# A two-block transformer kernel on one core: expert choosing paced by VectorE's estimated lead, cut into two-head pieces, and expert weighing handed out one chunk sooner

## The chip, the cores and the metric

The kernel runs on one core of one Trainium2 chip. The metric is device time in microseconds (us); the time of a kernel is the median of its runs. The engines are TensorE (PE: matmuls; PEld: its weight loads), VectorE (DVE), ScalarE (ACT), GpSimd (POOL) and SyncE (SP), which here only issues the loads of weights. TensorE's granted clock is shown as a share of its full 2.4 GHz.

## The reference

The reference computes two transformer blocks on 256 tokens of width 2048 in fp32. The change touches the feed-forward part of the first block, a layer of 16,384 experts from which each of 8 heads chooses 16 per token:

```python
def peer(x, w_query, sub_keys, expert_down, expert_up):
    q = (xt @ w_query).reshape(T, PEER_HEADS, 2, PEER_HALF)
    scores = jnp.einsum('thpc,hpnc->thpn', q, sub_keys)
    vals, idx = lax.top_k(scores, PEER_TOPK)
    cand = (vals[..., 0, :, None] + vals[..., 1, None, :]).reshape(T, PEER_HEADS, 256)
    top_vals, top_c = lax.top_k(cand, PEER_TOPK)
    i1 = jnp.take_along_axis(idx[..., 0, :], top_c // PEER_TOPK, axis=-1)
    i2 = jnp.take_along_axis(idx[..., 1, :], top_c % PEER_TOPK, axis=-1)
    experts = (i1 * PEER_N_KEYS + i2).reshape(T, PEER_HEADS * PEER_TOPK)
    gates = jax.nn.softmax(top_vals, axis=-1)
    ...
        u = jnp.take(expert_down, ec, axis=0)
        hdn = jax.nn.gelu(jnp.einsum('ted,td->te', u, xc))
        return jnp.einsum('te,ted->td', gc * hdn, jnp.take(expert_up, ec, axis=0))
```

## The kernel before, in words

**Dense experts.** The kernel does not gather experts. It computes gelu(x · expert_down) for all 16,384 experts, multiplies it by a gate that is zero where an expert wasn't chosen, and multiplies the product by expert_up. Every weight matrix is streamed once from HBM, and TensorE works through them in one long list of matmul stages.

**Steps.** A weight tile of 1 MB (`raw`, 3 buffers, loaded by SP) is worked in two halves. One half is a *step*, the variable `s` of the loop in `run` (L265); this text numbers steps by it. An fp32 product is made of three products of rounded operands, so each half is split: ScalarE copies it to `whi` (rounded), VectorE subtracts `raw - whi` into `wlo`. Both have 4 buffers, and the split of step s + 3 (`LOOK = 3`) is issued in step s. TensorE then runs the matmuls of step s. The query projection of the expert layer is steps 128 to 159; the expert_down stage, called s1, has 16 chunks of 1024 experts and is steps 160 to 415; the expert_up stage, s2, is steps 416 to 671. A step has 12 wide matmuls (512 columns) in the query stage and in s2, and the equal of 16 in s1.

**Evacuations.** Every 4 steps of s1 the accumulator is full and `s1_evac` (L919) empties it: ScalarE copies (`tmp<-acc`), VectorE adds and multiplies (`tmp<-tmp,acc`, `tmp<-tmp,nb`), ScalarE applies gelu and issues a store to HBM (`act`). These are issued at the end of steps 163, 167, ..., 415. The next steps' `whi` stand behind the gelu in ScalarE's order, and the `wlo` behind them.

**Side work.** The order of instructions on every engine is the order in which the program issues them. Work beside the matmuls is written as generators in named *lanes*; at the end of every step, `round` (L222) advances each running generator of each lane by one piece. The lanes that matter here:

- "top": `query` (L975) for a group of two heads and 128 tokens: transposes, key scores, and `top16` of 128 scores for two heads and two halves (MAX8, FIND_INDEX8, MATCH_REPLACE8 on VectorE).
- "choose": `choose` (L1016), for 4 heads and 128 tokens: candidate sums (14 small adds), top16 of 50 candidates, then for each head two pieces of compare, multiply and reduce over 128x400 to recover the ids (`eq`), and a softmax with one Exp on ScalarE. There are 4 of these.
- "rows": `scatter` (L1084). For each of 64 columns of a `choose`, GpSimd issues an indirect DMA that adds gates into one of four gate tensors in HBM (two halves of the heads, two of the tokens). There are 256 in all.
- "main": `weigh` (L1112), once per chunk. It waits, while the program is being written, until all scatters are issued, three of seven 8 KB `nb` buffers are free and it is at most one chunk ahead of the last one that was finished. Then GpSimd issues the loads of the chunk's activations and of four gate pieces and adds the head halves (`nb<-nb,nb`, 2 adds); after 5 rounds VectorE multiplies activations by gates (2 multiplies), and the result is split into the operand `xt` of s2.

The first `weigh` is handed to its lane at the last evacuation of chunk 14 (step 399).

**Estimates.** `Meter` (L171) adds up an estimated time `vt` for every engine as instructions are issued, kept from falling more than 2.0 us behind TensorE's. In `split`, a `wlo` is put on GpSimd instead of VectorE when VectorE's estimate leads:

```python
busy = self.vt["DVE"] - self.vt["PE"] > self.share and self.vt["POOL"] - self.vt["PE"] < 1.0
```

`share` is 2.0, and out of reach (1e9) from the first scatter issued to the last.

Of the kernel before, what the change touches and what calls it, by code (L numbers as in the profile page):

```python
# [8 lines left out]
F32 = mybir.dt.float32  # L9
# [4 lines left out]
OP = mybir.AluOpType  # L14
# [11 lines left out]
NCAND = 50  # L26
CLAMP = 2.0
SWA_ORDER = [0, 3, 1, 4, 2, 5, 6, 9, 7, 10, 8, 11]

# [142 lines left out]
class Meter:  # L172
# [5 lines left out]
    def __getattr__(self, op):  # L178
        f = getattr(self.eng, op)
        if "dma" in op or op == "preload_act_table_set":  # L180
            return f

        def g(*a, **k):
            out = a[0] if a else k["out"]
            n = 1
            for d in out.shape[1:]:
                n *= d
            per = self.per
            if self.name == "PE" and k.get("rhs", a[2] if len(a) > 2 else out).dtype == F32 and op == "matmul":
                per = 4 * per  # L190
            vt = self.vt
            vt[self.name] = max(vt[self.name], vt["PE"] - CLAMP if self.name != "PE" else 0.0) + self.fixed + n * per
            return f(*a, **k)  # L193
        return g


class Engines:
    def __init__(self, nc):
        self.vt = vt = dict(PE=0.0, DVE=0.0, ACT=0.0, POOL=0.0)
        self.tensor = Meter(nc.tensor, "PE", vt, 0.0, 0.000417)  # L200
        self.vector = Meter(nc.vector, "DVE", vt, 0.085, 0.00104)
        self.scalar = Meter(nc.scalar, "ACT", vt, 0.2, 0.00083)
        self.gpsimd = Meter(nc.gpsimd, "POOL", vt, 0.1, 0.00225)
        self.sync = nc.sync


class Build:
# [6 lines left out]

    def lane(self, name, width, starts=1):

        self.lanes[name] = dict(width=width, starts=starts, queue=deque(), active=[])

# [3 lines left out]
    def round(self):  # L222
        for ln in self.lanes.values():
            st = 0
            while ln["queue"] and len(ln["active"]) < ln["width"] and st < ln["starts"]:
                ln["active"].append([self.now, ln["queue"].popleft()])
                st += 1
            for item in list(ln["active"]):
                if item[0] <= self.now:
                    try:  # L230
                        w = next(item[1])
                        item[0] = self.now + (1 if w is None else w)
                    except StopIteration:
                        ln["active"].remove(item)
        self.now += 1
# [338 lines left out]
    def body(self):  # L574
        from contextlib import ExitStack
        with ExitStack() as ctx:
# [16 lines left out]
            self.lane("attn", 2, 1)  # L593
            self.lane("top", 1, 1)
            self.lane("choose", 1, 1)
            self.lane("rows", 4, 2)
# [285 lines left out]
    def peer(self, hn, st):  # L882
        nc, ins = self.nc, self.ins
# [23 lines left out]
        def q_evac(g, acc):  # L907
            for tt in range(2):
                self.until(lambda: st["q"])
                q = st["q"].popleft()  # L910
                nc.scalar.activation(q, acc[tt], AF.Copy, scale=st["rh"][:, tt:tt + 1])
                self.add("top", self.query(g, tt, q, st, topn))
            if g % 2:
                for tt in range(2):
                    self.add("choose", self.choose(g // 2, tt, st, topn, done))

        def s1_evac(c):
            def f(g, acc):
# [11 lines left out]
                if j == 3:  # L930
                    ws.append(self.weigh(c, acts, at, st, done, s2))
                    if c >= nch - 2:
                        while ws:
                            self.add("main", ws.pop(0))
# [80 lines left out]

    def choose(self, hf, tt, st, topn, done):  # L1016

        nc, p = self.nc, self.pp
        while (2 * hf, tt) not in topn or (2 * hf + 1, tt) not in topn:
            yield 1  # L1020
        hs = slice(4 * hf, 4 * hf + 4)
# [3 lines left out]
        cand = p.tile([128, 2, 4, NCAND], F32, name="cand", tag="cand", bufs=1)  # L1025
        ec = cand[:, 1]
        cand = cand[:, 0]
        eng = nc.vector
        for src, dst in ((v, cand), (ixf, ec)):
            o = 0  # L1030
            for a, na, nb in CAND:
                x0 = src[:, :, 0, a:a + na]
                x1 = src[:, :, 1, 0:nb]
                d = dst[:, :, o:o + na * nb]
                if na == 1:
                    eng.tensor_tensor(d, x0.to_broadcast([128, 4, nb]), x1, op=OP.add)
                elif nb == 1:
                    eng.tensor_tensor(d, x0, x1.to_broadcast([128, 4, na]), op=OP.add)
                else:
                    eng.tensor_tensor(d.rearrange("p h (a b) -> p h a b", a=na),  # L1040
                                      x0[:, :, :, None].to_broadcast([128, 4, na, nb]),
                                      x1[:, :, None, :].to_broadcast([128, 4, na, nb]), op=OP.add)
                o += na * nb
        yield 1
        tt4 = p.tile([128, 6, 4, 16], F32, name="tt4", tag="tt4", bufs=1)
        tv, tf, tp, e, gs = tt4[:, 0], tt4[:, 1], tt4[:, 2].bitcast(U32), tt4[:, 3], tt4[:, 4]
        for h in range(4):
            self.top16(cand[:, h, :], tv[:, h, :], tp[:, h, :])
            yield 1
        nc.vector.tensor_copy(tf, tp)  # L1050

        cs = slice(64 * hf, 64 * hf + 64)
        gt = st["pk"][:, tt, 1, cs].rearrange("p (h j) -> p h j", h=4)
        nc.vector.tensor_tensor(gt, tv, tv[:, :, 0:1].to_broadcast([128, 4, 16]), op=OP.subtract)
        nc.scalar.activation(gt, gt, AF.Exp)
# [7 lines left out]
        for h in range(4):  # L1063
            for j in (slice(0, 8), slice(8, 16)):
# [9 lines left out]
        nc.vector.reciprocal(gs[:, :, 1], gs[:, :, 0])  # L1074
        nc.vector.tensor_tensor(gt, gt, gs[:, :, 1:2].to_broadcast([128, 4, 16]), op=OP.mult)
# [4 lines left out]
        if hf == 1 and tt == 1:  # L1080
            self.nb.give(st["top"])
        self.add("rows", self.scatter(hf, tt, st, done))

    def scatter(self, hf, tt, st, done):  # L1084

        nc = self.nc
        gd = st["gd"][hf, tt].rearrange("e (t o) -> (e t) o", o=1)
# [6 lines left out]
        done["rows"] += 64  # L1094
        if done["rows"] == T:
# [16 lines left out]
    def weigh(self, c, acts, at, st, done, s2):  # L1112
# [592 lines left out]
```

## Time and profile before

| | us |
|---|---|
| median of 3 runs | 3170.18 (3170.11 to 3171.86) |
| the profiled execution, its own time | 3169.29 |
| its span in the trace | 3167.5 |
| TensorE busy in the span | 3076.1 (97%) |
| query projection, about | 460 to 545 |
| s1, about | 545 to 1328 |
| s2, from | 1328 |

Rows of the trace are read so: a row of instructions has the line, engine, operation, `out<-in` by the program's names, the count, then busy time and mean duration, and last the idle time of that engine just before, with what ended it. In a timeline the first number is the start in us, the second how long the group took. A row of waits says which engine waited, in which line, for whom, how long in total, how often and how long at most. Nearly all operations are recorded under one line (L193), as they pass through a helper, so the names of tiles tell them apart.

### The profile page before, as it was taken

To read this page: it belongs to the slowest core of one execution; us is meant where nothing else is said; L and a number is where in the kernel's file an instruction comes from. 1 tells how busy PE (TensorE), PEld (TensorE's weight loads), DVE (VectorE), ACT (ScalarE), POOL (GpSimd) and SP (SyncE) were. 2 spreads that over 40 slices of the span, in tenths; PEclk is the share of its full clock that TensorE was granted. 3 is DMA by queue.
4 is the path that set the end of the run, shared out by engine and by line. 5 is a ranking of instruction groups with operands and counts; after the bars stand their busy time and mean duration, and the time that the engine had idled before them with its cause. 6 is when DMAs were issued, how large, how long until landed. Compare 5 with 4: busy or idle time off the path is not lost.

```text
span 3167.5 us, 38904 instructions
## 1 busy us (share of the span) xinstructions
PE 3076.1 (97%) x15388; PEld 2576.2 (81%) x15388; DVE 2019.2 (64%) x2821; ACT 1438.3 (45%) x1908; POOL 748.2 (24%) x502
## 2 busy tenths in 40 slices
PE   8999999789999999789999999999999999999998
PEld 6888888678888888668888888877888888888887
DVE  5555667997555555657777765655757555555565
ACT  4444454444444444424444444554555444444444
POOL 3011200267888863433122200000111000000000
PEclk9999999999999999989999999999999999999999
DMA  9556954457777777778777755554444455555554
GB/s 348 216 178 222 330 180 173 137 165 201 209 211 211 212 210 241 279 264 280 263 269 267 278 203 187 185 203 139 170 172 169 172 192 188 194 190 186 189 194 149
DMA packets 157527, 667.28 MB, mean 211 GB/s; under 512 B 48945, under 2 KB 65757, under 8 KB 90145
## 3 DMA queue, kind: packets, MB, share of 16 engines
q1 hardware_dynamic: 77984, 551.64, 48.5%
q0 software_dynamic: 61808, 96.32, 12.4%
q10 hardware_dynamic: 17552, 16.85, 1.6%
q8 instruction: 120, 1.97, 0.2%
q14 instruction: 63, 0.51, 0.0%
HBM read 612.16 MB, written 54.94 MB: 211 GB/s over the span
## 4 chain that ended last, share of the span: by engine, by line
PE 86%; DVE 7%; DMA 3%; ACT 2%; issue 1%; POOL 1%; ACTq 0%; DVEq 0%; SPq 0%; POOLq 0%
PE acc L193 81%; PE aux L193 5%; DVE wlo L193 3%; DMA nb<-gates 2%; DVE nb L193 1%; ACT whi L193 1%; DVE tt L193 1%; DVE tmp L193 1%; DVE eq L193 1%; POOL nb L193 0%; DVE xt L193 0%; ACT tmp L193 0%; DMA raw<-in_w 0%; POOL nb L1121 0%; DMA raw<-in_wu 0%
## 5 line engine op out<-in xcount | busy, mean ns | idle before, releaser
L193 DVE TENSOR_TENSOR wlo<-raw,whi 128x1024 fp32r<-128x1024 f32 x1039 | 1303.6, 1261 | 896.4 <-ACT whi L193 895.6
L193 PE MATMUL acc<-whi,xt 128*128 128x512 f32 x5248 | 1668.1, 394 | 1.9 <-ACT whi L193 1.6
L193 ACT ACTIVATE whi<-raw 128x1024 fp32r<-128x1024 f32 x1040 | 1088.3, 1056 | 1052.8 <-PE acc L193 969.8
L193 PEld LDWEIGHTS acc<-whi,xt 128*128 128x128 f32 x5248 | 987.9, 188 | 215.3 <-issue 6.0
L193 PE MATMUL acc<-xt,whi 128*128 128x512 f32 x3072 | 1086.3, 400 | 1.0 <-DVE xt L193 1.0
L193 PE MATMUL acc<-wlo,xt 128*128 128x512 f32 x2624 | 1025.1, 391 | 21.6 <-DVE wlo L193 11.4
L193 PE MATMUL acc<-xt,wlo 128*128 128x256 f32 x3072 | 853.5, 283 | 45.7 <-DVE wlo L193 44.0
L193 PEld LDWEIGHTS acc<-xt,whi 128*128 128x128 f32 x3072 | 576.2, 189 | 133.8 <-DVE xt L193 1.2
L193 PEld LDWEIGHTS acc<-xt,wlo 128*128 128x128 f32 x3072 | 584.6, 190 | 61.7 <-DVE wlo L193 51.3
L193 PEld LDWEIGHTS acc<-wlo,xt 128*128 128x128 f32 x2624 | 494.7, 189 | 124.7 <-DVE wlo L193 14.3
L1090 POOL DMA_INDIRECT gates<-nb x256 | 476.5, 1861 | 413.3 <-DVE nb L193 231.4
L193 POOL TENSOR_TENSOR nb<-nb,nb 128x1024 f32<-128x1024 f32 (+1 forms) x34 | 98.1, 2901 | 197.2 <-DMA nb<-gates 172.6
L193 ACT ACTIVATE tmp<-tmp 128x512 f32<-128x512 f32 (+5 forms) x84 | 46.5, 554 | 179.4 <-DVE tmp L193 179.2
L1121 POOL DMA_DIRECT2D nb<-gates x64 | 56.9, 921 | 146.5 <-DVE xt L193 93.7
L193 ACT ACTIVATE tmp<-acc 128x256 f32<-128x256 f32 x128 | 47.1, 385 | 90.6 <-PE acc L193 90.6
L193 DVE TENSOR_TENSOR h<-h,acc 128x512 f32<-128x512 f32 x136 | 86.8, 679 | 0.0
L193 ACT ACTIVATE p<-p 128x128 f32<-128x128 f32 x88 | 39.4, 449 | 81.7 <-DVE p L193 81.7
L193 DVE TENSOR_TENSOR nb<-nb,nb 128x1024 f32<-128x1024 f32 (+2 forms) x42 | 61.2, 1465 | 23.6 <-POOL nb L193 23.6
L193 ACT ACTIVATE xt<-aux 128x512 fp32r<-128x512 f32 (+2 forms) x70 | 40.1, 583 | 79.4 <-PE aux L193 77.6
L193 DVE TENSOR_TENSOR tmp<-tmp,acc 128x256 f32<-128x256 f32 x128 | 49.2, 419 | 25.9 <-ACT tmp L193 25.9
L193 POOL TENSOR_TENSOR tmp<-nb,const 128x64 f32<-128x64 f32 x32 | 11.2, 379 | 229.4 <-ACT nb L193 229.4
L193 DVE TENSOR_TENSOR xt<-nb,xt 128x1024 fp32r<-128x1024 f32 x48 | 58.5, 1221 | 8.8 <-ACT xt L193 8.8
(232 smaller groups left out, 1253.4 us busy)
## 6 DMA issues: line engine op xcount, KB each, us to landing
raw<-in_wd SPq DMA_DIRECT2D x128, 1024.0 KB
raw<-in_wu SPq DMA_DIRECT2D x128, 1024.0 KB
raw<-in_wm SPq DMA_DIRECT2D x128, 1024.0 KB
raw<-in_w SPq DMA_DIRECT2D x87, 1024.0 KB
gates<-const POOLq DMA_DIRECT2D x32, 1024.0 KB
raw<-in_wo SPq DMA_DIRECT2D x32, 1024.0 KB
nb<-gates POOLq DMA_DIRECT2D x64, 512.0 KB
raw<-in_wq SPq DMA_DIRECT2D x16, 1024.0 KB
```

What stands on the lines that cost most here:

```text
L193: return f(*a, **k)
L1090: nc.gpsimd.indirect_dma_start(out=gd, out_offset=bass.IndirectOffsetOnAxis(ap=st["pk"][:, tt, 0, c:c + 1].bitcast(I32), axis=0), in_=st[" ...
L1121: nc.gpsimd.dma_start(g[:, :, 128 * tt:128 * tt + 128], st["gd"][hf, tt][CH * c:CH * c + CH].rearrange("(a p) t -> p a t", p=128))
```

## The change

1. **Estimates.** The size counted for an instruction is the largest of its operands instead of its output's. Each matmul gets 0.0133 us on top; VectorE's fixed and per-column estimates change slightly, and `max_index` and `match_replace` get 0.09 us on top.
2. **Pausing.** Lanes can be `paced`: their generators are not advanced in a round in which VectorE's estimate leads TensorE's by more than 2.0 us. "choose" and "top" are paced; "choose" now comes first, and "top" may run two generators.
3. **Choosing for two heads.** `choose` takes the two heads of one query group instead of four, so that there are 8 of them, each followed by 32 scatters instead of 64.
4. **Weighing.** The first `weigh` is handed out at the end of chunk 13 (step 383) instead of 14, and `weigh` waits 9 rounds instead of 5 between GpSimd's adds and VectorE's multiplies.

```diff
+MATCH, PACE = 0.09, 2.0
...
-            out = a[0] if a else k["out"]
             n = 1
-            for d in out.shape[1:]:
-                n *= d
+            for x in (a[:1] or (k["out"],)) if self.name == "PE" else (*a, *k.values()):
+                if len(getattr(x, "shape", ())) > 1:
+                    n = max(n, math.prod(x.shape[1:]))
...
+            vt[self.name] += MATCH if op in ("max_index", "match_replace") else 0.0
...
-        self.tensor = Meter(nc.tensor, "PE", vt, 0.0, 0.000417)
-        self.vector = Meter(nc.vector, "DVE", vt, 0.085, 0.00104)
+        self.tensor = Meter(nc.tensor, "PE", vt, 0.0133, 0.000417)
+        self.vector = Meter(nc.vector, "DVE", vt, 0.08, 0.00113)
...
-                if item[0] <= self.now:
+                if item[0] <= self.now and not (ln["paced"] and self.vt["DVE"] - self.vt["PE"] > PACE):
...
-            self.lane("top", 1, 1)
-            self.lane("choose", 1, 1)
+            self.lane("choose", 1, 1, True)
+            self.lane("top", 2, 2, True)
...
-            if g % 2:
-                for tt in range(2):
-                    self.add("choose", self.choose(g // 2, tt, st, topn, done))
+                self.add("choose", self.choose(g, tt, st, topn, done))
...
-                    if c >= nch - 2:
+                    if c >= nch - 3:
...
-    def choose(self, hf, tt, st, topn, done):
+    def choose(self, g, tt, st, topn, done):
...
-        while (2 * hf, tt) not in topn or (2 * hf + 1, tt) not in topn:
+        while (g, tt) not in topn:
...
-        for h in range(4):
+        for h in range(2):
...
-        for c in range(64 * hf, 64 * hf + 64):
+        for c in range(32 * g, 32 * g + 32):
...
-        yield 5
+        yield 9
```

Three places show what it moves in the orders of the engines.

**GpSimd, from the last zeroing of the gates to the first scatters** (`wlo` is the split of a weight half; `gates_188` and `gates_189` are two of the four gate tensors). Before, and then with the change:

```order
L896 DMA nb_12_3629<-in_keys 128x2048
L1108 DMA gates_191<-const 2048x1x128
L1090 DMA gates_188<-nb_14_3632 2097152x1 x15
L1090 DMA gates_189<-nb_14_3632 2097152x1
L1090 DMA gates_188<-nb_14_3632 2097152x1
```

```order
L1109 DMA gates_191<-const 2048x1x128
L195 TENSOR_TENSOR wlo<-raw,whi 128x1024 x7
L1091 DMA gates_188<-nb_14_3632 2097152x1 x9
L1091 DMA gates_189<-nb_14_3632 2097152x1
L1091 DMA gates_188<-nb_14_3632 2097152x1
```

Seven splits have moved from VectorE to GpSimd, ahead of its first scatter (they are issued in steps 139 to 141 and 146 to 149). The first scatter is issued in step 150 instead of 169, the last in step 258 instead of 278.

**VectorE, around an evacuation in s1 while choosing goes on** (`eq`, `cand` and `tt` belong to `choose`; `tmp` to the evacuation, `wlo` to the splits). Before, and then with the change:

```order
L193 TENSOR_TENSOR wlo<-raw,whi 128x1024
L193 TENSOR_TENSOR tmp<-tmp,acc 128x256 x2
L193 TENSOR_TENSOR tmp<-tmp,nb_14_3632 128x512
L193 TENSOR_REDUCE tt_4335<-eq_5_4546 128x8
L193 TENSOR_TENSOR eq_7_4616<-const,tt_4335 128x400
L193 TENSOR_TENSOR eq_7_4616<-eq_7_4616,cand 128x400
L193 TENSOR_TENSOR wlo<-raw,whi 128x1024
```

```order
L195 TENSOR_REDUCE tt_5296<-eq_18_5424 128x8
L195 TENSOR_TENSOR eq_20_5480<-const,tt_5296 128x400
L195 TENSOR_TENSOR eq_20_5480<-eq_20_5480,cand 128x400
L195 TENSOR_TENSOR wlo<-raw,whi 128x1024
L195 TENSOR_TENSOR tmp<-tmp,acc 128x256 x2
L195 TENSOR_TENSOR tmp<-tmp,nb_14_3632 128x512
L195 TENSOR_TENSOR wlo<-raw,whi 128x1024
```

Before, pieces of choosing stood between an evacuation and the next split; now the split follows at once. Of the 15 evacuations of steps 163 to 219, 1 was followed by a split at once before, and 12 are now. The last `choose` ends in step 227 instead of 215.

**VectorE, at the first multiplies of `weigh`** (`nb<-nb,nb`; `xt` is the operand of s2). Before, from the evacuation of step 403; with the change, from that of step 391:

```order
L193 TENSOR_TENSOR tmp<-tmp,acc 128x256 x2
L193 TENSOR_TENSOR tmp<-tmp,nb_14_3632 128x512
L193 TENSOR_TENSOR wlo<-raw,whi 128x1024
L193 TENSOR_TENSOR nb_15_10698<-nb_15_10698,nb_16_10699 128x1024
L193 TENSOR_TENSOR wlo<-raw,whi 128x1024
L193 TENSOR_TENSOR nb_15_10698<-nb_15_10698,nb_16_10699 128x1024
L193 TENSOR_TENSOR nb_18_10732<-nb_18_10732,nb_19_10733 128x1024
```

```order
L195 TENSOR_TENSOR tmp<-tmp,acc 128x256 x2
L195 TENSOR_TENSOR tmp<-tmp,nb_14_3632 128x512
L195 TENSOR_TENSOR wlo<-raw,whi 128x1024
L195 TENSOR_TENSOR nb_15_10421<-nb_15_10421,nb_16_10422 128x1024
L195 TENSOR_TENSOR wlo<-raw,whi 128x1024
L195 TENSOR_TENSOR nb_15_10421<-nb_15_10421,nb_16_10422 128x1024
L195 TENSOR_TENSOR nb_18_10455<-nb_18_10455,nb_19_10456 128x1024
```

The multiplies of chunks 0 and 1 stand three evacuations, 12 steps, sooner: they are issued in steps 392 to 394 instead of 404 to 406. Those of chunk 2 go to steps 404 and 405 (before: 412 and 413), those of chunks 3 and 4 to steps 424 to 427 (before: 420 to 423). The GpSimd parts of `weigh` are issued in steps 383, 384, 395, 415 and 417 (before: 399, 400, 407, 415 and 417). ScalarE issues 4 more table loads, since 8 Exps instead of 4 stand among the gelus. SP's order of loads is unchanged.

## Rows read from the trace of the kernel before

**Rows 1.** The page: busy time of each engine, share of the span, instructions.
```profile
PE 3076.1 (97%) x15388; PEld 2576.2 (81%) x15388; DVE 2019.2 (64%) x2821; ACT 1438.3 (45%) x1908; POOL 748.2 (24%) x502
```

**Rows 2.** The page: the chain that ended last, by engine.
```profile
PE 86%; DVE 7%; DMA 3%; ACT 2%; issue 1%; POOL 1%; ACTq 0%; DVEq 0%; SPq 0%; POOLq 0%
```

**Rows 3.** What TensorE waited for, whole span: total, times, longest.
```profile
PE acc L193 <- DVE wlo L193: 55.4, 26, 10.2
```

**Rows 4.** The same waits, from 560 to 760 us only.
```profile
PE acc L193 <- DVE wlo L193: 32.2, 20, 2.9
```

**Rows 5.** The same waits, from 1270 to 1420 us only.
```profile
PE acc L193 <- DVE wlo L193: 22.8, 5, 10.2
PE acc L193 <- POOL wlo L193: 10.3, 1, 10.3
```

**Rows 6.** Windows: stretch, length, busy time of each engine, granted clock, DMA share, GB/s.
```profile
600.00:650.00 50.00, 41.83 (x229) 35.38 (x230) 44.75 (x118) 21.67 (x30) 18.41 (x11) 0.97 0.52 155
1000.00:1050.00 50.00, 50.00 (x285) 43.44 (x285) 27.57 (x31) 25.39 (x32) 42.94 (x23) 1.00 0.73 197
1300.00:1350.00 50.00, 33.62 (x161) 27.65 (x161) 42.25 (x36) 21.09 (x25) 25.25 (x17) 0.88 0.77 268
1350.00:1400.00 50.00, 38.90 (x151) 31.39 (x152) 22.43 (x17) 13.08 (x13) 20.09 (x15) 0.83 0.75 252
1600.00:1650.00 50.00, 50.00 (x222) 41.42 (x221) 33.84 (x31) 21.52 (x21) 9.47 (x7) 1.00 0.77 270
```

**Rows 7.** ScalarE's timeline: evacuations at the ends of steps 163, 219, 395.
```profile
556.51 0.64 ACT L193 ACTIVATE tmp<-acc 128x256 f32<-128x256 f32 x2
...
761.13 0.73 ACT L193 ACTIVATE tmp<-acc 128x256 f32<-128x256 f32 x2 [1.25 <-PE acc L193]
...
1257.75 0.74 ACT L193 ACTIVATE tmp<-acc 128x256 f32<-128x256 f32 x2 [1.42 <-PE acc L193]
```

**Rows 8.** Groups of instructions by form.
```profile
L193 DVE TENSOR_TENSOR wlo<-raw,whi 128x1024 fp32r<-128x1024 f32 x1039 | 1303.6, 1261 | 896.4 <-ACT whi L193 895.6
...
L1090 POOL DMA_INDIRECT gates<-nb x256 | 476.5, 1861 | 413.3 <-DVE nb L193 231.4 <-DMA gates<-nb 127.7 <-issue 54.2
...
L193 ACT ACT_TABLE_LOAD x7 | 9.0, 1283 | 0.5 <-ACT tmp L193 0.4
...
L193 POOL TENSOR_TENSOR wlo<-raw,whi 128x1024 fp32r<-128x1024 f32 x1 | 3.3, 3317 | 0.0
```

**Rows 9.** VectorE's timeline: the 14 candidate adds of one choose.
```profile
591.81 1.46 DVE L193 TENSOR_TENSOR cand<-nb 128x64 f32<-128x64 f32 x14
```

**Rows 10.** VectorE's timeline, from the end of s1 into s2.
```profile
1261.87 1.23 DVE L193 TENSOR_TENSOR wlo<-raw,whi 128x1024 fp32r<-128x1024 f32 x1 [2.20 <-ACT whi L193]
...
1285.59 1.22 DVE L193 TENSOR_TENSOR nb<-nb,nb 128x1024 f32<-128x1024 f32 x1
...
1300.40 3.35 DVE L193 TENSOR_TENSOR nb<-nb,nb 128x1024 f32<-128x1024 f32 x1 [9.87 <-POOL nb L193]
...
1375.66 3.34 DVE L193 TENSOR_TENSOR nb<-nb,nb 128x1024 f32<-128x1024 f32 x1 [13.70 <-POOL nb L193]
...
1413.40 1.28 DVE L193 TENSOR_TENSOR h<-h,acc 128x512 f32<-128x512 f32 x2
```

**Rows 11.** GpSimd's timeline: scatters, loads and adds of weigh, one split.
```profile
588.99 2.40 POOL L1090 DMA_INDIRECT gates<-nb  x1 [231.10 <-DVE nb L193]
...
1246.14 1.58 POOL L1090 DMA_INDIRECT gates<-nb  x1 [2.60 <-DMA gates<-nb]
1247.16 1.54 POOL L1118 DMA_DIRECT2D nb<-act  x1
...
1269.67 5.21 POOL L193 TENSOR_TENSOR nb<-nb,nb 128x1024 f32<-128x1024 f32 x2 [17.41 <-DMA nb<-gates]
...
1298.03 4.63 POOL L193 TENSOR_TENSOR nb<-nb,nb 128x1024 f32<-128x1024 f32 x2 [18.79 <-DMA nb<-gates]
...
1348.24 3.32 POOL L193 TENSOR_TENSOR wlo<-raw,whi 128x1024 fp32r<-128x1024 f32 x1
```

More of the change, by code (lines that the diff above doesn't have):

```diff
@@ L212, in __init__, with lane @@
         self.now = 0
-    def lane(self, name, width, starts=1):
-        self.lanes[name] = dict(width=width, starts=starts, queue=deque(), active=[])
+    def lane(self, name, width, starts=1, paced=False):
+        self.lanes[name] = dict(width=width, starts=starts, paced=paced, queue=deque(), active=[])
     def add(self, lane, gen):
@@ L1014, in top16 @@
         nc.vector.max_index(out=ix[:, 8:16], in_max=v[:, 8:16], in_values=a)
[L1016 removed]
+    def choose(self, g, tt, st, topn, done):
         nc, p = self.nc, self.pp
[L1019 removed]
+        while (g, tt) not in topn:
             yield 1
[L1021 removed]
+        hs = slice(2 * g, 2 * g + 2)
         v, ixf = st["v"][:, tt, hs], st["ixf"][:, tt, hs]
@@ L1024, in choose @@
         nc.vector.tensor_scalar(ixf[:, :, 0, :], ixf[:, :, 0, :], 128.0, None, op0=OP.mult)
-        cand = p.tile([128, 2, 4, NCAND], F32, name="cand", tag="cand", bufs=1)
+        cand = p.tile([128, 2, 2, NCAND], F32, name="cand", tag="cand", bufs=1)
         ec = cand[:, 1]
@@ L1035, in choose @@
                 if na == 1:
-                    eng.tensor_tensor(d, x0.to_broadcast([128, 4, nb]), x1, op=OP.add)
+                    eng.tensor_tensor(d, x0.to_broadcast([128, 2, nb]), x1, op=OP.add)
                 elif nb == 1:
-                    eng.tensor_tensor(d, x0, x1.to_broadcast([128, 4, na]), op=OP.add)
+                    eng.tensor_tensor(d, x0, x1.to_broadcast([128, 2, na]), op=OP.add)
                 else:
                     eng.tensor_tensor(d.rearrange("p h (a b) -> p h a b", a=na),
-                                      x0[:, :, :, None].to_broadcast([128, 4, na, nb]),
-                                      x1[:, :, None, :].to_broadcast([128, 4, na, nb]), op=OP.add)
+                                      x0[:, :, :, None].to_broadcast([128, 2, na, nb]),
+                                      x1[:, :, None, :].to_broadcast([128, 2, na, nb]), op=OP.add)
                 o += na * nb
         yield 1
-        tt4 = p.tile([128, 6, 4, 16], F32, name="tt4", tag="tt4", bufs=1)
+        tt4 = p.tile([128, 6, 2, 16], F32, name="tt4", tag="tt4", bufs=1)
         tv, tf, tp, e, gs = tt4[:, 0], tt4[:, 1], tt4[:, 2].bitcast(U32), tt4[:, 3], tt4[:, 4]
-        for h in range(4):
+        for h in range(2):
             self.top16(cand[:, h, :], tv[:, h, :], tp[:, h, :])
@@ L1050, in choose @@
         nc.vector.tensor_copy(tf, tp)
-        cs = slice(64 * hf, 64 * hf + 64)
-        gt = st["pk"][:, tt, 1, cs].rearrange("p (h j) -> p h j", h=4)
-        nc.vector.tensor_tensor(gt, tv, tv[:, :, 0:1].to_broadcast([128, 4, 16]), op=OP.subtract)
+        cs = slice(32 * g, 32 * g + 32)
+        gt = st["pk"][:, tt, 1, cs].rearrange("p (h j) -> p h j", h=2)
+        nc.vector.tensor_tensor(gt, tv, tv[:, :, 0:1].to_broadcast([128, 2, 16]), op=OP.subtract)
         nc.scalar.activation(gt, gt, AF.Exp)
@@ L1062, in total @@
             self.eqs.give(eq)
-        for h in range(4):
+        for h in range(2):
             for j in (slice(0, 8), slice(8, 16)):
@@ L1074, in choose @@
         nc.vector.reciprocal(gs[:, :, 1], gs[:, :, 0])
-        nc.vector.tensor_tensor(gt, gt, gs[:, :, 1:2].to_broadcast([128, 4, 16]), op=OP.mult)
+        nc.vector.tensor_tensor(gt, gt, gs[:, :, 1:2].to_broadcast([128, 2, 16]), op=OP.mult)
         for x in held:
@@ L1079, in choose, with scatter @@
         nc.vector.tensor_scalar(ix, e.rearrange("p a b -> p (a b)"), 128.0, self.c("row"), op0=OP.mult, op1=OP.add)
-        if hf == 1 and tt == 1:
+        if g == 3 and tt == 1:
             self.nb.give(st["top"])
-        self.add("rows", self.scatter(hf, tt, st, done))
-    def scatter(self, hf, tt, st, done):
+        self.add("rows", self.scatter(g, tt, st, done))
+    def scatter(self, g, tt, st, done):
         nc = self.nc
-        gd = st["gd"][hf, tt].rearrange("e (t o) -> (e t) o", o=1)
+        gd = st["gd"][g % 2, tt].rearrange("e (t o) -> (e t) o", o=1)
         self.share = 1e9
-        for c in range(64 * hf, 64 * hf + 64):
+        for c in range(32 * g, 32 * g + 32):
             nc.gpsimd.indirect_dma_start(
@@ L1093, in scatter @@
             yield 1
-        done["rows"] += 64
+        done["rows"] += 32
         if done["rows"] == T:
```

## The prediction

> **What bounds the kernel now.** I read the page first: TensorE is busy for 3076.1 of 3167.5 us [rows 1], and the chain that ended last is 86% TensorE, 7% VectorE and 3% DMA [rows 2]. So only the places where TensorE stands still, or is clocked down, are to be won. The waits of TensorE say who causes them: VectorE's `wlo`, 55.4 us in 26 waits [rows 3]. By stretch, 32.2 us of these lie between 560 and 760 us [rows 4], where experts are chosen, and 22.8 us between 1270 and 1420 us, with 10.3 us more for the one `wlo` on GpSimd [rows 5], where s1 passes into s2. From 760 to 1270 TensorE doesn't wait: a window there is 50.00 of 50 [rows 6].
>
> The windows give the undisturbed step. In s1 285 matmuls take 50 us, so a step of 16 takes 2.81 us; in s2 222 take 50 us, so a step of 12 takes 2.70 us [rows 6].
>
> *Choosing.* The evacuations of steps 163 and 219 stand at 556.51 and 761.13 [rows 7]: 204.6 us for 56 steps, against 56 x 2.81 = 157.2. Of the 47.4 us over, 32.2 are the waits; the other 15 are the query's own transposes and key scores, and some clock (0.97). VectorE is busy for 44.75 of 50 us there [rows 6]: it is the bound.
>
> *Passing into s2.* From the evacuation of step 395 at 1257.75 [rows 7] to that of step 435 at 1413.40 [rows 10] it is 155.7 us, against 20 x 2.81 + 20 x 2.70 = 110.2: 45.5 us over. Of these 33.1 are waits [rows 5]; the rest fits the granted clock, 0.88 and 0.83 of 2.4 GHz in the two windows in which TensorE had been standing [rows 6]. The cause is a chain: the last scatter is issued at 1246.14, weigh 0 can only then load (1247.16), its add starts at 1269.67, that of weigh 1 at 1298.03 [rows 11]. VectorE stands at the multiply of weigh 1 for 9.87 us and at that of weigh 4 for 13.70 us [rows 10], with the next `wlo` behind it in its order.
>
> **The change, part by part.**
>
> *Scatters start sooner.* The first is issued in step 150 instead of 169. Step 150 ends 9 x 2.70 + 4 x 2.81 = 35.6 us before 556.51, at 521. Before, the first scatter ran at 588.99 [rows 11], 12 us behind its step, since VectorE was late; so it will run between 521 and 533, I take 527, with VectorE less crowded. GpSimd's seven splits stand ahead of it: 7 x 3.32 = 23 us [rows 8], issued over 11 steps (30 us), which covers them. The 256 scatters took (1246.14 - 588.99) / 255 = 2.58 us each from start to start [rows 8, 11]. The last `choose` ends at about step 227, near 790, and the 32 scatters behind it need 82 us, so choosing doesn't hold them up. The last scatter is then at 527 + 657 = 1184, 62 us sooner.
>
> *Multiplies stand 12 steps sooner.* The first half of weigh 1's add was ready 54.3 us behind the last scatter (1300.40, when the multiply began, less 1246.14): now at 1238. VectorE reached that multiply at 1300.40 - 9.87 = 1290.5; twelve steps sooner, with the 3 us found below, this is 1254. So weigh 0 and 1 cost no wait, with 16 us to spare. Weigh 2 needs a buffer that weigh 0's multiply gives back near 1250; 22.5 us from load to add (1247.16 to 1269.67) and half an add give 1275, against step 404 at about 1281: 6 us to spare. The one `wlo` of step 416 on GpSimd now stands behind weigh 3's add, which is done by 1312; its `whi` comes at about 1316, so it ends near 1319, when TensorE wants it at 1322. Before it ran at 1348.24 [rows 11]. Weigh 4 loads behind it, adds at 1342 and is half done at 1345, against multiplies at about 1342 to 1345 (step 426). Here a wait of 0 to 5 us remains, and the multiplies beside GpSimd's adds stay slow (3.35 against 1.22 us [rows 10]). I leave 4 us: **-41.5 us**. The bounds are -45.5 (nothing left) and about -20 (one of the two waits stays).
>
> *Choosing paused.* Pausing should make VectorE's work fit TensorE's time, but the estimate counts instructions, not gaps. After an evacuation VectorE stands for 2.20 us until ScalarE, behind its gelu, has made the next `whi` [rows 10]. Before, pieces of choosing filled that gap at 14 of 15 evacuations; now 12 of the 15 are followed by a split at once, since the evacuation itself lifts the estimate over the limit. While there is choosing left, VectorE works at the limit and doesn't make up what the estimate doesn't see. TensorE then waits for 12 x 2.20 = 26.4 us of gaps. Four more table loads of 1.28 us [rows 8] stand in ScalarE's way to `whi`; some lie under VectorE's own work, so of 5.1 us I take half. Together 29 us, against 32.2 now: **-3 us**. The Trainium skill, "ScalarE: Activation LUTs", section "What ACT_TABLE_LOAD costs", gives a switch of sets 2.66 us with its drain, and its rules say to do all of one set before switching, which eight chooses do less than four. Four switches by that figure are an estimated 10.6 us, and the sum would be some 8 us higher; the trace shows the 1.283 us load and no drain beside it.
>
> *More pieces.* Four more chooses repeat 22 small instructions each; 14 candidate adds took 1.46 us [rows 9], so 88 take 9.2 us. The last choose ends 12 steps later, where VectorE is busy for 27.57 of 50 us [rows 6], so this is covered: 0, at most 9.2. The seven splits taken off VectorE save it 7 x 1.26 = 8.8 us [rows 8] ahead of step 163, where TensorE hardly waits: 0. Both fall due in TensorE's waits if VectorE is late already in step 163.
>
> So choosing lies between -32 (gaps don't bind) and 26.4 + 5.1 + 9.2 + 6 - 32.2 = +14.5, the 6 being GpSimd's splits in VectorE's way (rival 2). The value is nearest to the row of the gap.
>
> **Sum.** The profiled execution took 3169.29 us, 0.9 under the median of the runs (0.03%). 3169.3 - 41.5 - 3 = 3124.8; on the median 3126.
>
> **The rivals.**
>
> 1. *Pausing works in full.* TensorE has splits three steps ahead, 8 us; if these take up the gaps, 29 us more go: 3097. For it: from 760 to 1270 every evacuation has the same gap and TensorE never waits. Against: there VectorE has 22 us of 50 to recover in, under choosing it hasn't.
>
> 2. *Choosing gets slower.* A multiply took 3.35 us beside GpSimd's add and 1.22 alone [rows 10]: 2.1 us lost. Seven splits on GpSimd beside the two-operand compares would cost VectorE 7 x 2.1 = 15 us and save 8.8, so +6; with all loads and pieces falling due choosing is at +14.5 instead of -3: 3143. The Trainium skill, "SBUF — State Buffer", section "Who interferes with whom", says that a VectorE instruction with two SBUF inputs and a GpSimd instruction reading SBUF exclude one another for a whole instruction. By that rule up to 3.3 us would be lost for each, an estimated 23 us instead of 15; the row shows 2.1. Against the rival: these splits lie ahead of step 150, where TensorE hardly waits.
>
> 3. *One wait stays in the passage.* Weigh 2 has 6 us to spare and weigh 4 none; if the loads take some 10 us longer beside s1's weights, about 20 us come back: 3146.
>
> 4. *Slower.* The multiplies now stand in VectorE's order 12 steps (33 us) sooner, whether the scatters are done or not, with all splits behind them. Each us by which the last scatter passes 1184 + 16 = 1200 is a us of TensorE's time. At 1244 the gain is gone, and beyond 1251 the kernel is slower by over 0.2%. That needs a mean of 2.84 us from scatter to scatter instead of 2.58, from the waits for an earlier scatter into the same tensor, such as the 2.60 us ahead of the last one [rows 11]: at 2.87 the last is at 1259 and the time 3185 at most, I say 3178. Against: the scatters' order over the tensors is hardly changed, and nothing else is on GpSimd.
>
> 5. *It doesn't do what it says.* VectorE is so late in the query stage that the scatters start near 580 after all: the last comes near 1240, and the time is 3166 to 3170.
>
> **How the numbers follow.** The forecast has 0.50, rival 1 0.15, rival 2 0.14, rival 3 0.10, rival 4 0.06, rival 5 0.05. The range reaches from rival 1 to rival 3 and takes in the bounds of the terms: 3096 to 3150, leaving out rivals 4 and 5. A change under 0.2% (6.3 us) can't be told from none here. Faster by more than that are the forecast and rivals 1 to 3, less a little for two mishaps together: 0.88. Same is rival 5 and a little of 4: 0.05; slower 0.07.
>
> **What would show it.** Right: the first scatter near 527 and the last near 1184; no VectorE wait for GpSimd at the multiplies of weigh 0 to 2; TensorE's waits from 1270 to 1420 under 6 us, its clock there near 1.00; between the evacuations of steps 163 and 219 some 200 us, with about 29 us of waits for `wlo`, now after bare evacuations. Wrong: choosing waits under 10 us (rival 1) or over 40 (rival 2); a wait over 10 us for GpSimd's add (rivals 3 and 4, told apart by the last scatter's start).

## The result, and the profile after

The changed kernel takes 3134.05 us (median of 4 runs, 3132.98 to 3135.41); the kernel before, run beside it, 3170.14. The ratio is 0.9886, with a 95% interval of 0.9872 to 0.9899: 36 us faster. The forecast was 3126, with a range of 3096 to 3150.

The page of the changed kernel, the same two lines as [rows 1] and [rows 2]:

```profile
PE 3073.2 (98%) x15388; PEld 2573.9 (82%) x15388; DVE 2010.8 (64%) x2902; ACT 1442.5 (46%) x1916; POOL 754.3 (24%) x509
...
PE 86%; DVE 9%; ACT 2%; DMA 2%; issue 1%; POOL 0%; ACTq 0%; DVEq 0%; SPq 0%; POOLq 0%
```

They hardly differ: busy shares of the whole span don't show where 35 us went (span 3132.4 after 3167.5). The waits by stretch do. TensorE's waits in the changed kernel, first from 460 to 800 us (choosing), then from 1240 to 1420 us (the passage into s2), against 32.2 us and 33.1 us in [rows 4, 5]:

```profile
PE acc L195 <- DVE wlo L195: 25.1, 20, 3.4
PE aux L195 <- ACT xt L195: 3.1, 1, 3.1
```

```profile
PE acc L195 <- DVE wlo L195: 4.9, 5, 3.4
PE acc L195 <- POOL wlo L195: 0.8, 1, 0.8
```

So choosing still stands for 28 us, and the passage has lost nearly all its waits. The windows say the same (columns as in [rows 6]); TensorE's granted clock in the passage is 1.00 and 0.97 of 2.4 GHz, where it was 0.88 and 0.83:

```profile
600.00:650.00 50.00, 45.74 (x255) 38.70 (x254) 41.69 (x124) 22.03 (x30) 38.08 (x22) 1.00 0.60 149
1300.00:1350.00 50.00, 49.22 (x232) 40.64 (x231) 34.63 (x33) 23.67 (x27) 9.37 (x8) 1.00 0.77 275
1350.00:1400.00 50.00, 45.92 (x193) 36.84 (x192) 37.81 (x32) 18.31 (x18) 18.07 (x14) 0.97 0.82 287
```

Fixed points in time show what each stretch took. ScalarE's timeline of the changed kernel, the evacuations of steps 163, 219, 231 and 395 (compare [rows 7]):

```profile
564.11 0.64 ACT L195 ACTIVATE tmp<-acc 128x256 f32<-128x256 f32 x2
...
752.21 0.73 ACT L195 ACTIVATE tmp<-acc 128x256 f32<-128x256 f32 x2 [1.26 <-PE acc L195]
...
792.07 0.74 ACT L195 ACTIVATE tmp<-acc 128x256 f32<-128x256 f32 x2 [1.24 <-PE acc L195]
...
1254.64 0.74 ACT L195 ACTIVATE tmp<-acc 128x256 f32<-128x256 f32 x2 [1.42 <-PE acc L195]
```

Step 231 in the kernel before, and step 467, where both kernels run evenly again, in the kernel before and in the changed one:

```profile
794.99 0.74 ACT L193 ACTIVATE tmp<-acc 128x256 f32<-128x256 f32 x2 [1.42 <-PE acc L193]
...
1496.58 1.28 DVE L193 TENSOR_TENSOR h<-h,acc 128x512 f32<-128x512 f32 x2
```

```profile
1461.85 1.28 DVE L195 TENSOR_TENSOR h<-h,acc 128x512 f32<-128x512 f32 x2
```

By step 219 the changed kernel is 8.9 us ahead (761.13 - 752.21), by step 231 only 2.9, by step 395 3.1, and by step 467 34.7. So the passage gave 31.6 us of the 35, choosing 3, and choosing gave back 6 of the 9 us that it had won, between steps 219 and 231, where only the changed kernel still chooses.

GpSimd's timeline of the changed kernel shows the chain behind the passage (compare [rows 11]): first and last scatter, adds of weigh 0 to 3, the one split, first load and add of weigh 4.

```profile
528.36 1.71 POOL L1091 DMA_INDIRECT gates<-nb  x1 [8.27 <-DVE nb L195]
...
1175.50 1.55 POOL L1091 DMA_INDIRECT gates<-nb  x1 [2.65 <-DMA gates<-nb]
...
1200.03 5.80 POOL L195 TENSOR_TENSOR nb<-nb,nb 128x1024 f32<-128x1024 f32 x2 [18.44 <-DMA nb<-gates]
...
1228.84 5.88 POOL L195 TENSOR_TENSOR nb<-nb,nb 128x1024 f32<-128x1024 f32 x2 [18.67 <-DMA nb<-gates]
...
1265.76 5.87 POOL L195 TENSOR_TENSOR nb<-nb,nb 128x1024 f32<-128x1024 f32 x2 [9.83 <-DMA nb<-gates]
...
1294.97 5.73 POOL L195 TENSOR_TENSOR nb<-nb,nb 128x1024 f32<-128x1024 f32 x2 [19.00 <-DMA nb<-gates]
1321.77 3.23 POOL L195 TENSOR_TENSOR wlo<-raw,whi 128x1024 fp32r<-128x1024 f32 x1 [21.06 <-ACT whi L195]
1324.94 0.89 POOL L1119 DMA_DIRECT2D nb<-act  x1
...
1348.91 4.73 POOL L195 TENSOR_TENSOR nb<-nb,nb 128x1024 f32<-128x1024 f32 x2 [19.57 <-DMA nb<-gates]
```

The adds of weigh 0 and 1 are done by 1235, before VectorE reaches their multiplies at 1248.62. From 1240 to 1420 only one multiply still waits for GpSimd, that of weigh 4:

```profile
1351.34 3.38 DVE L195 TENSOR_TENSOR nb<-nb,nb 128x1024 f32<-128x1024 f32 x1 [4.64 <-POOL nb L195]
```

### The profile page after: what moved, and what is told of

Read it like the earlier page. It is cut to its first block, busy times and chain, and to the rows that moved or that the text cites. A ratio compares the mean times of both kernels' runs of the same rounds, so it can differ in the third digit from the quotient of the medians.

```text
span 3132.4 us, 39007 instructions
## 1 busy us (share of the span) xinstructions
PE 3073.2 (98%) x15388; PEld 2573.9 (82%) x15388; DVE 2010.8 (64%) x2902; ACT 1442.5 (46%) x1916; POOL 754.3 (24%) x509
## 4 chain that ended last, share of the span: by engine, by line
PE 86%; DVE 9%; ACT 2%; DMA 2%; issue 1%; POOL 0%; ACTq 0%; DVEq 0%; SPq 0%; POOLq 0%
PE acc L195 80%; PE aux L195 5%; DVE wlo L195 4%; DVE nb L195 1%; ACT whi L195 1%; DVE tmp L195 1%; DVE tt L195 1%; DVE eq L195 1%; DMA nb<-gates 1%; ACT tmp L195 1%; DVE xt L195 1%; DMA raw<-in_wu 0%; DVE cand L195 0%; DMA raw<-in_w 0%; ACTq L930 0%
## 5 line engine op out<-in xcount | busy, mean ns | idle before, releaser
L1091 POOL DMA_INDIRECT gates<-nb x256 | 464.4, 1814 | 192.6 <-DMA gates<-nb 131.9
L195 ACT ACTIVATE xt<-nb 128x1024 fp32r<-128x1024 f32 x48 | 50.3, 1053 | 32.1 <-PE acc L195 31.2
```

Of the source, the lines that this page charges most:

```text
L1091: nc.gpsimd.indirect_dma_start(out=gd, out_offset=bass.IndirectOffsetOnAxis(ap=st["pk"][:, tt, 0, c:c + 1].bitcast(I32), axis=0), in_=st[" ...
```

## The experiments

| kernel | us, median | ratio to before, 95% interval |
|---|---|---|
| changed | 3134.05 | 0.9886 (0.9872 to 0.9899) |
| e1: weigh's part alone | 3174.82 | 1.0013 (1.0003 to 1.0022) |
| e2: all but weigh's part | 3151.78 | 0.9941 (0.9924 to 0.9958) |
| e7: changed, no pausing | 3141.05 | 0.9906 (0.9891 to 0.9921) |
| e8: changed, four-head chooses | 3176.76 | 1.0023 (1.0013 to 1.0032) |
| e3: changed, gap in the estimate | 3239.14 | 1.0223 (1.0206 to 1.0240) |
| e4: changed, gelu later | 3137.44 | 0.9898 (0.9881 to 0.9914) |
| e5: e4 with scatters spread | 3102.01 | 0.9785 (0.9772 to 0.9798) |
| e6: e3 with scatters spread | 3103.91 | 0.9788 (0.9773 to 0.9803) |
| e9: changed, scatters spread | 3135.97 | 0.9895 (0.9879 to 0.9911) |
| e10: changed, no early split on GpSimd | 3132.62 | 0.9884 (0.9868 to 0.9899) |
| e11: e5, no late split on GpSimd | 3094.12 | 0.9758 (0.9744 to 0.9772) |
| e12: changed, no late split on GpSimd | 3127.91 | 0.9867 (0.9850 to 0.9883) |

Each ratio is to the kernel before, run beside the kernel of that row; e12 ran on another chip than e1 to e11.

### Which part of the change gains: e1, e2, e7, e8

**e1** is the kernel before with `c >= nch - 3` and `yield 9`, nothing else.

> The kernel before with part 4 alone: first weigh handed out at step 383, 9 rounds before the multiplies. The scatters are not sooner, so the last one stays near 1246. Theory of the prediction (a multiply that stands sooner than its add only moves the wait forward): VectorE waits some 40 to 45 us at the multiply of weigh 1, and the time is that of the kernel before or slightly more, 3166 to 3182. Rival (the hand-out itself, with more rounds in between, is what pays): 3140 to 3150.

It is slower by a little. The last scatter came at 1253.54, and VectorE's timeline shows the wait split over the multiplies of weigh 0 and weigh 1:

```profile
1271.01 3.35 DVE L193 TENSOR_TENSOR nb<-nb,nb 128x1024 f32<-128x1024 f32 x1 [17.70 <-POOL nb L193]
...
1290.17 3.34 DVE L193 TENSOR_TENSOR nb<-nb,nb 128x1024 f32<-128x1024 f32 x1 [13.54 <-POOL nb L193]
```

It is 31 us, less than the 40 to 45 expected, as the loads landed sooner; TensorE waited for 36.6 us in the passage, against 33.1 before. Handing the work out sooner is worth nothing while its input isn't there.

**e2** is the changed kernel with `c >= nch - 2` and `yield 5`.

> The changed kernel without part 4: estimates, pausing and two-head chooses stay, weigh is handed out at step 399 with 5 rounds, as before. The last scatter comes near 1176 as in the changed kernel. Theory (both halves are needed: buffers of weigh 0 come free only at its multiply in step 405, so weigh 2 to 4 stay late): no wait at weigh 1, but 5 to 17 us each at weigh 3 or 4 and at the split on GpSimd; 3150 to 3160. Rival (only the end of the scatters counts): 3132 to 3140. In both the stretch up to step 395 is as in the changed kernel, 3 us shorter than before.

The last scatter came at 1169.80, yet TensorE waits 21.8 us in the passage. GpSimd's and VectorE's timelines show why: the gate loads of weigh 2 stand for a buffer that VectorE gives back only at its multiplies in steps 404 to 406, and the chain is late from there, up to weigh 4:

```profile
1288.12 3.52 POOL L1122 DMA_DIRECT2D nb<-gates  x4 [57.90 <-DVE nb L195]
...
1332.92 3.33 POOL L195 TENSOR_TENSOR wlo<-raw,whi 128x1024 fp32r<-128x1024 f32 x1
...
1360.36 3.35 DVE L195 TENSOR_TENSOR nb<-nb,nb 128x1024 f32<-128x1024 f32 x1 [14.86 <-POOL nb L195]
```

So weigh's part alone loses 4 us, the rest alone gains 19, and both together gain 36: the sooner scatters make the sooner multiplies free, and the sooner multiplies give back the buffers.

**e7** sets the limit out of reach (`PACE = 1e9`).

> The changed kernel without pausing (its limit out of reach); two-head chooses, estimates and weigh stay. Theory (pausing by this estimate gains little, since the gaps and a later end of choosing give back what it saves): waits for wlo from 460 to 800 of 32 to 42 us instead of 25, last scatter before 1180, time 3138 to 3148. Rival (pausing is what eases TensorE): over 3155.

Its waits from 460 to 800 are 31.4 us, its last scatter comes at 1148.88. By the medians, pausing is worth 7 us (3141.05 to 3134.05; the two intervals overlap a little), and it is paid for with scatters that end 27 us later, which here cost nothing.

**e8** has `choose` and `scatter` of the kernel before, all else as changed.

> The changed kernel with choosing for four heads at a time as before; pausing, estimates and weigh stay. Theory (the two-head pieces bring the gain, by starting the scatters some 40 us sooner and spreading them better over the tensors): first scatter near 565, last near 1250, a wait of some 40 us at weigh 1, time 3160 to 3175, although the waits under choosing are no more than in the changed kernel. Rival (the pausing and the hand-out bring it): 3130 to 3142.

The first scatter came at 578.25, 13 us later than expected, the last at 1249.96. VectorE waited 19.39 and 13.27 us at the multiplies of weigh 0 and weigh 1, TensorE's waits for `wlo` from 460 to 800 were 28.7 us, a little over the changed kernel's 25.1, and the time, 3176.76, lies 2 us above the expected range. Without the smaller pieces the whole gain is gone, and only 3.6 us of it lie in those waits. Of the 74 us by which the last scatter comes later than in the changed kernel, 50 are the later start, since the first piece is ready only after two groups of heads instead of one; the other 25 are a longer run of scatters (672 us from first to last instead of 647).

### What still stands under choosing: e3, e4, and what came in the way

**e4** hands gelu and store of an evacuation to a new first lane, one step later (the handing-out of `weigh` goes with them):

```diff
-                nc.scalar.activation(sg, sg, AF.Gelu_apprx_tanh)
-                nc.scalar.dma_start(acts[c][2 * j:2 * j + 2].rearrange("a p t -> p a t"), sg)
-                if j == 3:
...
+                self.add("late", self.late(c, j, sg, acts, ws, at, st, done, s2, nch))
...
+    def late(self, c, j, sg, acts, ws, at, st, done, s2, nch):
+        nc = self.nc
+        yield 1
+        nc.scalar.activation(sg, sg, AF.Gelu_apprx_tanh)
...
```

> The changed kernel, with gelu and store of an evacuation issued one step later, so that the next whi no longer stands behind them in ScalarE's order and VectorE has no gap behind the evacuation. Pausing and the order of VectorE's work stay. Theory (the gap is the cause): waits for wlo from 460 to 800 fall from 25.1 to under 10 us, and the time to 3108 to 3120. Rival (the work itself is too much, or the gelu was never in the way): 3128 to 3138 with the waits over 18.

**e3** adds the gap to the estimate: behind each evacuation, while scatters are still to be issued, `self.vt["DVE"] += 2.2`.

> The changed kernel, with VectorE's estimate raised by 2.2 us at each s1 evacuation while scatters are still to be issued, which is the gap that the estimate does not see; choosing then pauses more and ends at step 282 instead of 227. Theory (12 gaps of 2.2 us are what TensorE still waits for under choosing): its waits for wlo from 460 to 800, 25.1 us in the changed kernel, fall under 12, and the time to 3116 to 3124. Rival (VectorE is late there because its work is longer than estimated, or ScalarE's table loads hold the splits up): waits stay over 18 and the time is 3128 to 3138. The scatters should start as in the changed kernel and end no later than 1190.

e4's time, 3137, fits the rival, and e3's, 3239, fits neither. Yet the waits fell as the theory of the gap has it, from 25.1 to 7.0 us (e4, first row) and 5.5 us (e3):

```profile
PE acc L195 <- DVE wlo L195: 7.0, 5, 3.4
...
PE acc L195 <- DVE wlo L195: 5.5, 4, 3.4
```

e4 reached the evacuation of step 391 at 1213.51, 30 us before the changed kernel (1243.36). That is 9 us more than the waits that went, 18.1 for `wlo` and 3.1 behind ScalarE; the granted clock from 600 to 800 us was 1.00 instead of 0.98, and the rest is not taken apart. One evacuation on VectorE's timeline shows it, in the changed kernel and then in e4, where the 2.20 us are gone:

```profile
636.65 0.69 DVE L195 TENSOR_TENSOR tmp<-tmp,nb 128x512 f32<-128x512 f32 x1
639.54 1.24 DVE L195 TENSOR_TENSOR wlo<-raw,whi 128x1024 fp32r<-128x1024 f32 x1 [2.20 <-ACT whi L195]
```

```profile
639.01 0.69 DVE L195 TENSOR_TENSOR tmp<-tmp,nb 128x512 f32<-128x512 f32 x1
639.62 1.22 DVE L195 TENSOR_TENSOR wlo<-raw,whi 128x1024 fp32r<-128x1024 f32 x1
```

What was won there was lost in the passage, because the last scatter came later, in e4 and in e3:

```profile
1215.73 2.25 POOL L1086 DMA_INDIRECT gates<-nb  x1 [3.54 <-DMA gates<-nb]
...
1315.34 1.55 POOL L1093 DMA_INDIRECT gates<-nb  x1 [1.69 <-DMA gates<-nb]
```

TensorE waited 35.0 us in the passage in e4. In e3 VectorE stood 115.77 us at the first multiply, and a window shows TensorE at rest:

```profile
1250.00:1300.00 50.00, 0.00 (x0) 0.00 (x0) 0.00 (x0) 0.00 (x0) 24.05 (x16) 0.50 0.13 0
```

The table sorts the starts of all 256 scatters by how many others lie between one and the one before it into the same gate tensor (mean us from the scatter just ahead, and count):

| | none between | one | two or more | first to last, us |
|---|---|---|---|---|
| before | 4.41 x28 | 2.57 x72 | 2.25 x155 | 657 |
| changed | 4.65 x19 | 2.64 x82 | 2.22 x154 | 647 |
| e4 | 5.11 x19 | 2.86 x82 | 2.30 x154 | 686 |
| e3 | 4.14 x90 | 2.61 x116 | 2.24 x49 | 786 |

A scatter waits until the one before it into the same tensor has landed. In e3 choosing pauses so long that often only one generator has columns left.

**e5** and **e6** add one edit to e4 and e3: `yield 2` instead of `yield 1` behind each scatter, so that generators of different tensors overlap for longer.

> The kernel with the later gelu, whose choosing lost its waits but whose last scatter came at 1216 instead of 1176; now each scatter generator issues a column every second round instead of every round, so that more of them run side by side and fewer scatters follow one into the same gate tensor at a distance of one or two (from 19 and 82 to 9 and 20 of 255). Theory (a scatter waits for the landing of the one before it into the same tensor, 4 to 5 us when it follows directly, 2.6 to 2.9 with one between, 2.3 otherwise; and a last scatter later than 1200 is paid in full at the multiply of weigh 1): last scatter at 1120 to 1150, no wait at weigh 1, time 3106 to 3116. Rival (the scatters are slower because TensorE, running without pauses, draws more weights): last scatter still after 1190, time 3128 to 3138.

> The kernel with the gap in the estimate, 3239 us with its last scatter at 1315, with the same spread of the scatters (from 90 and 116 at a distance of one and two to 16 and 50). Theory (the order over the tensors made it slow): last scatter at 1140 to 1180, no wait at weigh 1, waits under choosing still under 8 us: 3106 to 3118. Rival (choosing, which ends at step 282, delivers its columns too late): last scatter after 1230 and time over 3150.

Both settle it for the order over the tensors: 3102 and 3104 us, each a little under its expected range, with 9 and 20 scatters at the two short distances in e5 and 16 and 50 in e6. The last scatters came at 1160.98 and 1159.64, and waits under choosing stayed at 6.7 and 5.3 us. The last scatter of e5 was 11 us later than expected.

**e9** is that edit on the changed kernel alone.

> The changed kernel with only the spread of the scatters (a column every second round), gelu as in the changed kernel. Theory (the changed kernel's last scatter at 1176 already costs no wait, so a sooner end is worth nothing, and the gain of the later gelu with the spread is the gaps'): last scatter at 1125 to 1150, waits for wlo from 460 to 800 still 22 to 28 us, time 3129 to 3138. Rival (the scatters still held the passage into s2 up): 3120 or less.

The last scatter came at 1128.39, 47 us sooner, and the time is the same within the intervals. In the changed kernel the end of the scatters costs nothing; it decides only once choosing is faster.

### GpSimd's splits: e10, e11, e12

Each bars GpSimd from splits in a range of steps. e12 does it on the changed kernel and e11 on e5, both with this edit:

```diff
-            (nc.gpsimd if busy and s > self.COLD else nc.vector).tensor_tensor(...)
+            (nc.gpsimd if busy and s > self.COLD and not 396 <= s < 432 else nc.vector).tensor_tensor(...)
```

**e10** is the changed kernel with `128 <= s < 160` in that place.

> The changed kernel with no split on GpSimd from step 128 to 159: the seven there go back to VectorE, and choosing pauses more (last choose in step 232 instead of 227). Theory (the seven are covered, worth 0): waits for wlo from 460 to 800 of 22 to 32 us, time 3131 to 3141. Rival 2 of the prediction (they cost VectorE more than they save, and cause the 3.4 us wait near 531): waits from 460 to 560 gone and 3126 or less.

The wait near 531 fell to 0.9 us and those from 460 to 800 to 22.5, but the time is within the interval of the changed kernel's: no difference that these runs can tell from 0, as forecast. What one such split can cost VectorE is seen in GpSimd's and VectorE's timelines of the changed kernel; this multiply of choosing takes 0.57 us otherwise:

```profile
514.96 2.39 POOL L195 TENSOR_TENSOR wlo<-raw,whi 128x1024 fp32r<-128x1024 f32 x1 [0.32 <-ACT whi L195]
...
515.11 2.67 DVE L195 TENSOR_TENSOR eq<-eq,cand 128x400 f32<-128x400 f32 x1
```

**e12** is the changed kernel without its one late split on GpSimd.

> The changed kernel itself with no split on GpSimd from step 396 to 431, which bears on the passage into s2: there 31.6 us were saved where 41.5 were forecast. In the changed kernel the one split stood 21.06 us for its whi, and the loads of weigh 4 behind it were issued at 1324.94, though weigh 3's add was done at 1300.7. Theory (this wait in GpSimd's order is what was left): VectorE's wait of 4.64 us at weigh 4 and TensorE's waits from 1240 to 1420 (5.7 us) vanish, and the time is 3125 to 3130. Rival (contention and buffers leave the rest): at most 2 us gained, 3132 to 3136.

TensorE's waits from 1240 to 1420 are down to this row, and no multiply waits for GpSimd:

```profile
PE acc L195 <- DVE wlo L195: 1.2, 3, 0.4
```

By the medians, 6 us of the changed kernel's 3134 were this one split (the two intervals overlap a little; the waits don't). It takes 3.23 us itself, but it stood 21.06 us in GpSimd's order with weigh 4's loads behind it. Without it the first of these, of the activations, is issued at 1302.39 instead of 1324.94. The gate loads then stand for VectorE (13.54 and 5.05 us), and the add starts 17 us sooner, at 1331.66 instead of 1348.91. GpSimd's timeline of e12:

```profile
1302.39 0.89 POOL L1119 DMA_DIRECT2D nb<-act  x1
1316.82 1.77 POOL L1122 DMA_DIRECT2D nb<-gates  x2 [13.54 <-DVE tmp L195]
1323.65 1.76 POOL L1122 DMA_DIRECT2D nb<-gates  x2 [5.05 <-DVE xt L195]
1331.66 5.75 POOL L195 TENSOR_TENSOR nb<-nb,nb 128x1024 f32<-128x1024 f32 x2 [6.25 <-DMA nb<-gates]
```

**e11** is e5 without its two late splits on GpSimd.

> The kernel with the later gelu and spread scatters, with no split on GpSimd from step 396 to 431. There two splits stood in GpSimd's order ahead of the loads of weigh 2 and weigh 4 and waited 11.42 and 4.69 us for their whi. Theory (this wait is why the adds of weigh 2 and 4 come late): VectorE's waits for them, 4.27 and 2.30 us, vanish, and the time falls from 3102 to 3095 to 3100. Rival (the buffers of the earlier weighs, given back by VectorE's multiplies, set when the loads start): the waits stay and the time is 3100 to 3105.

e11 is 3094.12 us, the best kernel of this study: 77 us under the kernel before and 40 under the changed one. It gains 8 us on e5, a little more than expected; the multiplies of weigh 2 and 4 no longer wait for GpSimd, and from 1180 to 1440 its TensorE has no wait. Its page:

```profile
PE 3060.0 (99%) x15388; PEld 2569.0 (83%) x15388; DVE 2008.6 (65%) x2903; ACT 1444.0 (47%) x1916; POOL 788.5 (25%) x508
```

## Why the prediction was right, point by point

**Scatters start sooner.** Forecast 527 for the first and 1184 for the last; measured 528.36 and 1175.50. Right, and e8 shows that it rests on the two-head pieces.

**Multiplies 12 steps sooner.** Forecast no wait at weigh 0 to 2: right. The size was off: -41.5 forecast, -31.6 measured (step 395 to step 467). Two things were mis-sized in this term. First, what was to be had. I took 45.5 us from an end point, step 435, whose evacuation was still late in the kernel before. Up to step 467 that kernel takes 1496.58 - 1257.75 = 238.8 us. The even pace there is 10.88 us per evacuation of 4 steps (13 of them), which with 20 steps of s1 makes 197.6: 41.2 us to be had. Second, what stays: 9.6 us instead of 4. I had the split of step 416 in GpSimd's order and its `whi` near 1316, and had it cost nothing. But its `whi` was ready only at 1321.77, weigh 4's loads took 24 us instead of 22.5, the multiply came 4.64 us late and took 3.38. e12 takes the split away: step 467 is then 199.8 us behind step 395, 2.2 over the even pace. That is 7.4 of the 9.6 us. The two steps in e12, on ScalarE's and VectorE's timelines:

```profile
1256.19 0.74 ACT L195 ACTIVATE tmp<-acc 128x256 f32<-128x256 f32 x2 [1.42 <-PE acc L195]
...
1455.94 1.28 DVE L195 TENSOR_TENSOR h<-h,acc 128x512 f32<-128x512 f32 x2
```

**Choosing paused.** Forecast -3, with 29 us of waits left because the estimate doesn't see the gap behind a bare evacuation; measured -3.1 up to step 395, with 25.1 us for `wlo` and 3.1 behind ScalarE. The mechanism is right, and e4 and e3 show it: without the gap, or with it in the estimate, 7.0 and 5.5 us are left.

That the sum came out to a tenth is luck, since its parts lay elsewhere. I put 26.4 us of gaps between steps 163 and 219, as if each of the twelve cost TensorE its full 2.20 us. All twelve are in the trace, but TensorE's waits there, from 560 to 760 us, are:

```profile
PE acc L195 <- DVE wlo L195: 17.9, 16, 1.8
```

In e4 3.6 us are left of these, so the gaps were worth some 14 us there, and 4 more from 760 to 800. I had the stretch from 163 to 219 at 200 us; it took 188.1, 16.5 less than before. Two things that I had put at nothing took most of that back. The evacuation of step 163 came 7.6 us later: just ahead of it ScalarE stood 7.36 us at an Exp of choosing, for VectorE in the crowded last steps of the query. And the stretch from 219 to 231, where I let the 9.2 us of added pieces be covered, took 39.9 us instead of 33.9, since the same gaps hold while choosing lasts. 16.5 less 7.6 less 6.0 makes the 3.

**Table loads.** I charged half of 5.1 us. They were worth next to nothing. Behind 10 of the 11 loads of the changed kernel ScalarE stands another 0.84 to 6.09 us for VectorE, so that the load lies in a wait that is there anyway; and in e4, where all 11 loads remain, the waits for `wlo` from 560 to 1000 us are 3.6 us in all. The 10.6 us that I estimated from the Trainium skill, "ScalarE: Activation LUTs", section "What ACT_TABLE_LOAD costs", are not seen in TensorE's time. Nor is a drain seen behind the one load after which ScalarE doesn't wait; its Exp follows at once:

```profile
772.79 1.28 ACT L195 ACT_TABLE_LOAD   x1 [0.43 <-ACT tmp L195]
774.09 0.23 ACT L195 ACTIVATE nb<-nb 128x32 f32<-128x32 f32 x1
```

**The rivals.** Rival 1 (the three steps that TensorE has in hand take up the gaps) did not happen: 25 us of waits stayed. Rival 2's price is real: the 2.67 instead of 0.57 us last until just behind the end of GpSimd's split. A whole GpSimd instruction is what the Trainium skill, "SBUF — State Buffer", section "Who interferes with whom", has it cost. But only two instructions of choosing met a split (the other took 2.02 us), some 3.5 us in all instead of 15, and e10 can't tell it from 0. Rival 3's sign, a wait over 10 us, did not show; weigh 4's wait of 4.64 us is within the forecast's own 0 to 5.

Rival 4's mechanism is real: e1 and e8 are slower by it, e3 by 68 us. Its price of a us for each us was right, and its deciding point, 1200, too early. I had taken 54.3 us from the last scatter to the multiply of weigh 1. The loads landed sooner: it was 37 us in e1 (1290.17 - 1253.54) and in e3 (1351.84 - 1315.34), and 41 in e4 (1256.47 - 1215.73), which puts the point 14 to 18 us later. It also moves with the rest: 3 us later in e1, where choosing was no faster, and 30 us sooner in e4 and 32 in e3, which reach the evacuation of step 391 at 1213.51 and 1211.66. The last scatter then came 33, 32 and 129 us behind the point in e1, e4 and e3, and TensorE waited 36.6, 35.0 and 128.9 us in the passage. A faster choosing uses up the room that the scatters had.

**Left open.** Why the same order of scatters took 39 us longer in e4 than in the changed kernel. From 600 to 800 us the DMA engines were busier (0.75 against 0.67 of the time, as TensorE drew its weights without pauses), and in e3, with DMA at 0.13, scatters followed each other at 3.3 us. That fits slower landings beside more traffic, but no run changed the traffic alone.

## What to carry to other kernels

An edit that moves a consumer ahead in an in-order engine and an edit that makes its input ready sooner are one change: run alone here, the first lost 4 us and the second gave 19 of the 36. Pace side work by an estimate that contains the gaps of the engine, not only its instructions, or remove the gap by moving what the next stage waits for ahead of the slow reply; then look again at what had been hidden by the old pace. Price work offloaded to a second engine by what stands behind it in that engine's order: one split of 3.2 us, which stood there for 21 us ahead of loads, cost about 6 us.

## What the runs showed of the hardware

In this program a scatter waits for the landing of the one before it into the same tensor. What I had not expected is how much of that the other tensors hide: starts follow each other at 2.2 to 2.3 us when two or more scatters to other tensors lie between, at 2.6 to 2.9 with one between, and at 4.1 to 5.1 with none (the four kernels of the table). Spreading the same 256 transfers over the four tensors took them from 786 us, first to last, to 629 (e3 to e6), and from 647 to 599 (the changed kernel to e9).
